# A hybrid attention and DeltaNet layer: the first attention unit's loads ahead of the last gates, bias rows in eight transfers, the output norm's power one part earlier, the gate rows' load pinned

## The chip, the cores and the metric

The kernel runs on one core of a Trainium2 chip. The metric is device time in microseconds (us), the median of three runs. An execution taken by the hardware profiler gives the trace from which all durations here are read. Engines: PE is TensorE (matmuls; PEld its weight loads), DVE is VectorE, ACT is ScalarE, POOL is GpSimd, and SP issues all the transfers.

## The reference

One layer over 2048 latent tokens and 256 context tokens, width 1024. One input projection feeds two branches that are merged at the end.

```
q, k, v, z  = NA projections ; o_na = softmax over (8 x 16 neighbourhood + 256 context keys), with a bias per head and offset
dq, dk, dv  = short conv, L2 norm, rotary ; o_dn, _ = gated delta rule, forward and backward, chunks of 64
u_na = (o_na * silu(z_na)) @ w_o_na
o_dn = rmsnorm(o_dn, dn_norm_w)
u_dn = (o_dn * silu(z_dn)) @ w_o_dn
y    = sigmoid(g_na) * u_na + sigmoid(g_dn) * u_dn
out  = x + gate * (y @ w_out)
```

## The kernel before

The work runs in stages. Projections, norms, the convolution and the triangular solves come first; their results go to DRAM tiles (names `d_...`). The last of the projections are the gates: `gate_units` multiplies a block of weights (`slots`) with all tokens (`hT`), squashes the sums on ACT (L207) and stores them to `d_g`. The last two gate blocks are done group by group of tokens in `gate_group(1)` to `gate_group(4)`. Between their matmuls run the first four steps of the DeltaNet scan (those of the context). When a group is done its part of `hT` is given back, and later pools lie in that memory.

After `gate_group(4)` a loop of 32 attention units begins, each for 128 queries of four heads. A unit computes scores by pairs of heads (`scores`, `scores_ctx`: L1051 adds the masks as a product with `mkr`, L1054 multiplies q with keys; L1068 on DVE adds the bias and takes the maximum; L1080 and L1083 on ACT exponentiate), turns the probabilities by PE (L1091, L1100) and multiplies with the values (L1111, L1115). The bias rows are in a DRAM tile `d_rp`, 16 shifted copies of the padded table, so that a plain two-dimensional read gives the right shift to each query; `load_bias` reads them for four heads with 32 transfers of 16 partitions.

One step of the scan is woven into each unit: `scan` is a generator, and `pump(chain, 1)` in the unit's code lets it run to its next `yield`, so five parts of it lie at fixed places in the unit. A step makes products with the state (L853), forms the new values (L857, L860, L871, copied to `cw` by L873), and updates the state (L867, L880, L883) and the output (L865, L882, L888). From the 17th latent step on both directions of a block of tokens are there: L865 adds the other direction's output, which lies in `os_`, and `dn_out` follows one step later. `dn_out` squares the block on ACT (L902), sums per head on DVE (L905, L906), raises to the power -1/2 on POOL (L908), multiplies by that on DVE (L909), transposes on PE (L913), multiplies by the gate rows `zd` on DVE (L914) and stores to `d_oz`. So `dn_out` lies in the last 15 units of the loop, and once after it.

The instructions of PE, and in the loop those of DVE, ACT and POOL, keep the order in which the code is written. SP's are placed by a scheduler, except where `keep_in_program_order` (`behind`) pins one against others pinned so. SP starts its transfers in that order, and each waits for the one eight before it, since eight semaphores go round. The order that matters most here, in `dn_out` and in the scan's step:

```
S.activation(ob, oa, AF.Square)
yield
V.reduce_sum(out=so, in_=ob, axis=AX.X)
V.tensor_scalar(out=so, in0=so, scalar1=4.0 / 64, scalar2=4.0 * EPS, op0=ALU.mult, op1=ALU.add)
G.tensor_tensor(out=ro, in0=so, in1=nh, op=ALU.pow)
V.tensor_tensor(out=oa, in0=oa, in1=ro.unsqueeze(2).to_broadcast([P, H, C]), op=ALU.mult)
yield
```

## Time and profile before

| what | value |
|---|---|
| median of 3 runs | 2374.77 us (2372.61 to 2375.72) |
| the profiled execution, its own time | 2373.14 us |
| its span, first to last instruction | 2371.4 us |
| PE busy in the span | 2162.9 us, 91% |
| mean granted TensorE clock, share of full speed | 0.959 |

The span is what the trace shows; 1.74 us of the execution's time lie outside it, and the median of the runs lies 1.63 us above that execution. Busy time is summed per engine; where PE is busy nearly all the time, its idle stretches and the stretches at the lower clock are what can be shortened. All times in the rows below are from the start of the span.

### The profile page before, as it was taken

To read this page: it belongs to the slowest core of one execution; us is meant where nothing else is said; L and a number is where in the kernel's file an instruction comes from. 1 tells how busy PE (TensorE), PEld (TensorE's weight loads), DVE (VectorE), ACT (ScalarE), POOL (GpSimd) and SP (SyncE) were. 2 spreads that over 40 slices of the span, in tenths; PEclk is the share of its full clock that TensorE was granted. 3 is DMA by queue.
4 is the path that set the end of the run, shared out by engine and by line. 5 is a ranking of instruction groups with operands and counts; after the bars stand their busy time and mean duration, and the time that the engine had idled before them with its cause. 6 is when DMAs were issued, how large, how long until landed. Compare 5 with 4: busy or idle time off the path is not lost.

```text
span 2371.4 us, 47485 instructions
## 1 busy us (share of the span) xinstructions
PE 2162.9 (91%) x18615; PEld 1814.3 (77%) x18615; DVE 1468.9 (62%) x2378; ACT 868.3 (37%) x2657; POOL 844.4 (36%) x712
## 2 busy tenths in 40 slices
PE   6999998998889999999999995899878876999999
PEld 2778777876667778999998874677766665889988
DVE  3736777559959969959679213666666774322222
ACT  4524343353433332344662113455444543211110
POOL 2514777644433112223432011211133334543442
PEclk8999999999999999999999997999888987999999
DMA  7323444665585252251443475777866664444342
GB/s 269 99 75 77 112 125 120 165 151 141 133 198 126 67 127 74 72 138 54 97 91 88 101 201 159 194 196 195 211 165 175 180 170 142 144 125 120 110 123 83
DMA packets 433480, 319.81 MB, mean 135 GB/s; under 512 B 200485, under 2 KB 361657, under 8 KB 432697
## 3 DMA queue, kind: packets, MB, share of 16 engines
q1 hardware_dynamic: 433256, 316.77, 50.3%
q8 instruction: 147, 2.41, 0.4%
q14 instruction: 77, 0.63, 0.1%
HBM read 206.24 MB, written 106.76 MB: 132 GB/s over the span
## 4 chain that ended last, share of the span: by engine, by line
PE 52%; DVE 18%; DMA 10%; POOL 8%; issue 7%; ACT 2%; SPq 2%; POOLq 0%; DVEq 0%; ACTq 0%
PE pd L181 19%; PE pf L1354 7%; PE pu L1343 7%; DVE Xs L584 6%; DVE tmp L582 6%; PE pd L731 5%; PE pw L1054 2%; PE pc L880 2%; PE pt L1091 1%; POOL rn L509 1%; PE pc L853 1%; POOL ro L908 1%; POOL xa L521 1%; PE po L1111 1%; PE pw L1051 1%
## 5 line engine op out<-in xcount | busy, mean ns | idle before, releaser
L181 PE MATMUL pd<-hT,slots 128*128 128x512 f32 (+1 forms) x3360 | 809.3, 395 | 1.9 <-ACT hT L321 1.6
L181 PEld LDWEIGHTS pd<-hT,slots 128*128 128x128 f32 x3360 | 617.0, 190 | 146.5 <-issue 3.8
L582 DVE TENSOR_TENSOR tmp<-Xs 128x236 f32<-128x236 f32 (+43 forms) x310 | 302.5, 976 | 36.8 <-DMA Xs<-d_X 28.1
L584 DVE TENSOR_TENSOR Xs<-Xs,tmp 128x236 f32<-128x236 f32 (+43 forms) x310 | 305.6, 986 | 8.4
L128 POOL TENSOR_TENSOR slots<-w_raw,slots 128x512 fp32r<-128x512 f32 (+1 forms) x76 | 114.1, 1501 | 379.8 <-ACT slots L127 379.7
L731 PE MATMUL pd<-slots,hT 128*128 128x256 f32 x1248 | 160.4, 288 | 0.0
L731 PE MATMUL pd<-wide,hT 128*128 128x256 f32 x1248 | 156.4, 287 | 2.4 <-ACT wide L127 1.4
L731 PEld LDWEIGHTS pd<-wide,hT 128*128 128x128 f32 x1248 | 153.6, 193 | 3.3 <-ACT wide L127 1.8
L731 PEld LDWEIGHTS pd<-slots,hT 128*128 128x128 f32 x1248 | 155.2, 191 | 0.0
L1344 DVE SCALAR_TENSOR_TENSOR gt<-gt,pu 128x256 f32<-128x256 f32 x120 | 46.5, 418 | 123.8 <-DMA gt<-d_g 65.3
L486 DVE SCALAR_TENSOR_TENSOR y<-raw,vT,y 128x512 f32<-128x512 f32 (+1 forms) x112 | 95.1, 860 | 25.5 <-ACT raw L474 21.4
L1068 DVE CUSTOM_DVE_ANT_1 pr<-pw,bias 128x288 f32<-128x288 f32 (+3 forms) x128 | 66.3, 553 | 69.5 <-PE pw L1054 69.5
L696 POOL TENSOR_TENSOR nrn<-nss,nhalf 128x8 f32<-128x8 f32 x34 | 71.5, 2102 | 104.8 <-DVE nss L695 104.8
L1080 ACT ACTIVATE pr<-pr,nm 128x288 f32<-128x288 f32 (+3 forms) x128 | 77.9, 609 | 81.3 <-DVE nm L1077 81.2
L207 ACT ACTIVATE zt<-pd 128x512 f32<-128x512 f32 x73 | 43.4, 594 | 150.7 <-PE pd L181 80.0
L1358 DVE SCALAR_TENSOR_TENSOR ckd<-pf,gate 128x512 f32<-128x512 f32 x32 | 22.0, 691 | 121.2 <-PE pf L1354 117.7
L1343 PE MATMUL pu<-ckq,OS 128*128 128x256 f32 x512 | 95.1, 284 | 0.9 <-DVE cv L1344 0.9
L1346 ACT CAST yh<-gt 128x256 fp32r<-128x256 f32 x60 | 24.3, 406 | 191.9 <-POOL gt L1345 191.9
L1345 POOL TENSOR_TENSOR gt<-gt 128x256 f32<-128x256 f32 x60 | 45.0, 750 | 126.3 <-DVE gt L1344 123.5
L1102 ACT COPY pTc<-pt 128x512 f32<-128x512 f32 x64 | 37.5, 586 | 137.9 <-PE pt L1100 137.9
L867 POOL TENSOR_TENSOR sd<-sd,gts 128x512 f32<-128x512 f32 x36 | 40.0, 1111 | 129.8 <-PE pc L853 121.9
L127 ACT CAST slots<-w_raw 128x512 fp32r<-128x512 f32 (+1 forms) x76 | 46.4, 611 | 106.6 <-DMA w_raw<-in_w_in_dram 85.1
(299 smaller groups left out, 4647.9 us busy)
## 6 DMA issues: line engine op xcount, KB each, us to landing
w_raw<-in_w_in_dram SPq DMA_DIRECT2D x92, 256.0 KB
ckq<-d_kq SPq DMA_DIRECT2D x64, 256.0 KB
gt<-d_g SPq DMA_DIRECT2D x60, 256.0 KB
d_g<-zt SPq DMA_DIRECT2D x41, 256.0 KB
d_X<-X SPq DMA_DIRECT2D x72, 128.0 KB
Xs<-d_X SPq DMA_DIRECT2D x18, 512.0 KB
cv<-d_v SPq DMA_DIRECT2D x72, 128.0 KB
cT<-d_T SPq DMA_DIRECT2D x72, 128.0 KB
```

The lines of the kernel that those rows point to most:

```text
L128: G.tensor_tensor(out=lo[:, j:j + 4, 0:n], in0=wr, in1=hi[:, j:j + 4, 0:n].bitcast(F32), op=ALU.subtract)
L181: PE.matmul(ps[0:n, 0:m], a[:, k, 0:n], h_part(g, z, k), start=k == 0 and i == 0, stop=k == KB - 1 and i == 2)
L486: V.scalar_tensor_tensor(out=y[:, 0:m], in0=raw[:, o + j - 1:o + j - 1 + m], scalar=tap(j), in1=y[:, 0:m], op0=ALU.mult, op1=ALU.add)
L582: V.tensor_tensor(out=tv, in0=X[r, piv, cols].unsqueeze(1).to_broadcast([8 * n, m, w]), in1=X[r, rows, piv].unsqueeze(2).to_broadcast([8 * ...
L584: V.tensor_tensor(out=X[r, rows, cols], in0=X[r, rows, cols], in1=tv, op=ALU.add)
L696: G.tensor_tensor(out=rn, in0=ss, in1=nhalf, op=ALU.pow)
L731: PE.matmul(ps[:, 256 * i:256 * i + 256], h[:, 256 * j + P * i:256 * j + P * i + P], w[:, :, part, k, :], start=k == 0 and n == 0, stop=k ...
L880: PE.matmul(p4[half[d], h, :], ld["ckd"][half[d], h, :], w[half[d], h, :], start=True, stop=True)
L1068: V.tensor_tensor_reduce(rc(self.e[u][:, 0:nk]), rc(pws[u][:, 0:nk]), biases[self.hg][:, 2 * pr + u, k0:k0 + self.nr, w0:w0 + w], 1.0, -3. ...
L1080: S.activation(e[:, 0:nk], e[:, 0:nk], AF.Exp, bias=nm[:, u:u + 1], accum_out=self.sums[:, hh, 0:1])
L1343: PE.matmul(ps, a, r[:, k, :], start=k == 0 and n == 0, stop=k == 3 and n == 2)
L1354: PE.matmul(ps, a[:, k, P * i:P * i + P], b[k, n], start=k == 0 and m == 0, stop=k == KB - 1 and m == 2)
```

## The change

Four edits.

1. The loads of the first attention unit (`load_q(0)`, the masks `k_mk`, `att_load(0)`, the context values `vc`) and the casts of q and masks are written ahead of `gate_group(4)`. q and masks use the staging tile `oa` (`raw0`) in place of `fwr`, which lies in memory that is given back only after the gates. The bias rows stay behind `gate_group(4)`.
2. `d_rp` gets longer rows, so that one transfer can take four heads: eight transfers of 16 x 4 x 752 elements in place of 32 of 16 x 752, for each half of the heads.
3. In `dn_out` the `yield` moves from ahead of the sum to behind the power: sum and power are done one part earlier, the multiplication stays. In the scan's step the addition L865 moves behind L867 (L868 and L866 in the changed kernel).
4. The load of `zd` is pinned in program order.

```diff
-    d_rp = dram.tile([16, RL + 47], F32, name="d_rp")
+    RW = RL + 8 * 47
+    d_rp = dram.tile([16, RW], F32, name="d_rp")
...
-                if i - CCH >= 16:
-                    G.tensor_tensor(out=tq.rearrange("p h e -> p (h e)"), in0=tq.rearrange("p h e -> p (h e)"), in1=os_[:, NCH - 1 - i], op=ALU.add)
                 yield
             G.tensor_tensor(out=sd, in0=sd, in1=gts[:, i].unsqueeze(2).to_broadcast([P, H, C]), op=ALU.mult)
+            if main and i - CCH >= 16:
+                G.tensor_tensor(out=tq.rearrange("p h e -> p (h e)"), in0=tq.rearrange("p h e -> p (h e)"), in1=os_[:, NCH - 1 - i], op=ALU.add)
...
-                    SP.dma_start(out=zd, in_=d_z[1, :, :, P * (i - CCH - 16):P * (i - CCH - 15)].rearrange("p q t -> q p t"))
+                    tc.keep_in_program_order(SP.dma_start(out=zd, in_=d_z[1, :, :, P * (i - CCH - 16):P * (i - CCH - 15)].rearrange("p q t -> q p t")))
...
             S.activation(ob, oa, AF.Square)
-            yield
             so = q2.tile([P, H], F32, name="so", bufs=2)
...
             G.tensor_tensor(out=ro, in0=so, in1=nh, op=ALU.pow)
+            yield
             V.tensor_tensor(out=oa, in0=oa, in1=ro.unsqueeze(2).to_broadcast([P, H, C]), op=ALU.mult)
...
-            for h in range(4):
-                for qr in range(8):
-                    if qr % 4 == 0:
-                        yield z
-                    o = ((4 * hg + h) * 23 + 7 - qr) * 47
-                    behind(SP.dma_start(out=z[16 * qr:16 * qr + 16, h].rearrange("q k w -> q (k w)"), in_=skew[:, o:o + 16 * 47]))
+            for qr in range(8):
+                yield z
+                o = (4 * hg * 23 + 7 - qr) * 47
+                rows = skew[:, o:o + 4 * 23 * 47].rearrange("q (h w) -> q h w", h=4)[:, :, 0:16 * 47]
+                behind(SP.dma_start(out=z[16 * qr:16 * qr + 16].rearrange("q h k w -> q h (k w)"), in_=rows))
...
+        q_split = load_q(0)
+        mkraw = ap_("fwr").rearrange("p b t -> p (b t)")[:, 0:432]
+        SP.dma_start(out=mkraw, in_=k_mk)
+        first = att_load(0)
+        SP.dma_start(out=vc, in_=d_nv[0:TC].rearrange("(b q) e -> q b e", q=P))
+        q_split()
+        mkr = aq.tile([P, 432], F32R, name="mkr")
+        S.copy(mkr, mkraw)
+        gate_group(4)
...
-        first = att_load(0)
-        SP.dma_start(out=vc, in_=d_nv[0:TC].rearrange("(b q) e -> q b e", q=P))
         bias_load = load_bias(0)
...
-        mkraw = ap_("fwr").rearrange("p a b -> p (a b)")[:, 0:432]
-        SP.dma_start(out=mkraw, in_=k_mk)
-        mkr = aq.tile([P, 432], F32R, name="mkr")
-        S.copy(mkr, mkraw)
-        load_q(0)()
```

What this does to the queues is seen at three places. The first is SP's queue at the end of the gates. Before, the masks and the first q stand behind all 32 bias transfers:

```order
L1019 DMA azt<-d_z 128x2x512
L213 DMA d_g<-co 128x512
L834 DMA cv<-d_v 64x512
L835 DMA cT<-d_T 64x512
L834 DMA cv<-d_v 64x512
L835 DMA cT<-d_T 64x512
L975 DMA bias<-d_rp 16x752 x2
L213 DMA d_g<-zd 128x512
L975 DMA bias<-d_rp 16x752 x30
L1221 DMA fwr<-in_k_mk_dram 128x432
L951 DMA fwr<-d_nq 128x2x256
L951 DMA fwr<-d_nk 128x2x256
```

In the changed kernel SP issues q and masks (L952, L1029, into `oa`) some twenty transfers earlier, ahead of the first unit's other loads:

```order
L836 DMA cT<-d_T 64x512
L952 DMA oa<-d_nq 128x2x256
L1029 DMA oa<-in_k_mk_dram 128x432
L214 DMA d_g<-ob 128x512
L1012 DMA azt<-d_z 128x2x512
L1017 DMA vt<-d_nv 96x1x256 x3
L1031 DMA vc<-d_nv 128x2x512
L837 DMA ckd<-d_kd 64x512 x2
```

And further on in the same queue, where the 32 transfers stood, it has eight, behind the first loads for later units:

```order
L1012 DMA azt<-d_z 128x2x512
L835 DMA cv<-d_v 64x512
L836 DMA cT<-d_T 64x512
L835 DMA cv<-d_v 64x512
L836 DMA cT<-d_T 64x512
L952 DMA fwr<-d_nk 128x2x256
L952 DMA fwr<-d_nq 128x2x256
L214 DMA d_g<-zd 128x512
L975 DMA bias<-d_rp 16x4x752 x8
L837 DMA ckd<-d_kd 64x512 x2
```

So the masks and q have moved ahead of the bias rows, and the bias rows stay last. The second place is DVE in a unit of the loop that has `dn_out` in it. Before, the sums L905 and L906 follow the maximum over the context keys (L1075, L1077):

```order
L857 TENSOR_TENSOR cr<-pc,egw 128x512
L1075 TENSOR_REDUCE mx<-pw 128x1 x2
L1077 TENSOR_REDUCE nm<-mx 128x2
L905 TENSOR_REDUCE so<-ob 128x8
L906 TENSOR_SCALAR so<-so 128x8
L909 TENSOR_TENSOR co<-co,ro 128x512
L914 SCALAR_TENSOR_TENSOR zd<-pc,vT,zd 128x512
```

In the changed kernel (line numbers 1 to 9 higher) they stand ahead of it:

```order
L858 TENSOR_TENSOR cr<-pc,egw 128x512
L905 TENSOR_REDUCE so<-ob 128x8
L906 TENSOR_SCALAR so<-so 128x8
L1084 TENSOR_REDUCE mx<-pw 128x1 x2
L1086 TENSOR_REDUCE nm<-mx 128x2
L910 TENSOR_TENSOR co<-co,ro 128x512
L915 SCALAR_TENSOR_TENSOR zd<-pc,vT,zd 128x512
```

Three small DVE instructions now come between the sums and the multiplication. The third place is POOL in the same unit. Before, the power L908 stands behind the scan's two operations:

```order
L1123 COPY rb<-ri 128x256
L865 TENSOR_TENSOR cr<-cr,OS 128x512
L867 TENSOR_TENSOR sd<-sd,gts 128x512
L908 TENSOR_TENSOR ro<-so,nh 128x8
L955 TENSOR_TENSOR ql<-fwr,qh 128x512
```

In the changed kernel it stands ahead of both, and these two have changed places:

```order
L1132 COPY rb<-ri 128x256
L908 TENSOR_TENSOR ro<-so,nh 128x8
L866 TENSOR_TENSOR sd<-sd,gts 128x512
L868 TENSOR_TENSOR cr<-cr,OS 128x512
L956 TENSOR_TENSOR ql<-fwr,qh 128x512
```

What followed the power directly, here a split of q (L955) or in other units nothing, has moved behind two operations more. PE's order is the same in both kernels up to the final projections. The load of `zd`, which before stood twice at the start of the loop and from then on was always two blocks ahead, now stands one block ahead, at the end of the step that makes the block.

## Rows read from the trace of the kernel before

**Rows 1.** The page, part 1: busy us (share of the span) and instructions

```profile
PE 2162.9 (91%) x18615; PEld 1814.3 (77%) x18615; DVE 1468.9 (62%) x2378; ACT 868.3 (37%) x2657; POOL 844.4 (36%) x712
```

**Rows 2.** Windows: stretch, length, busy us per engine, granted clock, DMA share, GB/s

```profile
1420.00:1447.00 27.00, 2.56 (x19) 1.52 (x13) 1.22 (x4) 1.17 (x2) 1.30 (x1) 0.58 0.55 152
1447.00:1705.00 258.00, 231.54 (x4247) 183.87 (x4249) 165.81 (x447) 124.49 (x365) 47.66 (x50) 0.91 0.73 192
1705.00:1980.00 275.00, 219.89 (x3939) 180.04 (x3934) 196.07 (x458) 128.77 (x361) 94.92 (x87) 0.90 0.66 172
```

**Rows 3.** Timeline of PE, end of gates: start, length, line, out<-in, [idle before <-releaser]

```profile
1418.98 1.15 PE L880 MATMUL pc<-cw,ckd 64*64 64x64 f32 x32
1443.70 0.85 PE L1051 MATMUL pw<-mkr 64*128 64x288 f32 x4 [23.57 <-ACT mkr L1223]
```

**Rows 4.** Timeline of SP's issues, same place

```profile
1414.17 0.59 SPq L1019 DMA_DIRECT2D azt<-d_z  x1
...
1425.68 0.34 SPq L213 DMA_DIRECT2D d_g<-zd  x1
1426.07 14.24 SPq L975 DMA_DIRECT2D bias<-d_rp  x30
```

**Rows 5.** Timelines of ACT and of DVE, same place

```profile
1443.10 0.55 ACT L1223 CAST mkr<-fwr 128x432 fp32r<-128x432 f32 x1 [23.41 <-DMA fwr<-in_k_mk_dram]
...
1446.47 0.46 DVE L1068 CUSTOM_DVE_ANT_1 pr<-pw,bias 128x288 f32<-128x288 f32 x1 [25.53 <-PE pw L1054]
```

**Rows 6.** Windows at the same place, for the last column, GB/s

```profile
1418.00:1422.00 4.00, 2.13 (x37) 1.53 (x35) 0.69 (x1) 0.60 (x1) 0.00 (x0) 1.00 0.87 247
...
1434.00:1438.00 4.00, 0.00 (x0) 0.00 (x0) 0.00 (x0) 0.00 (x0) 0.00 (x0) 0.50 0.39 108
```

**Rows 7.** Waits, 1705 to 1990 us: us in total, times, longest

```profile
PE pc L913 <- DVE co L909: 53.6, 15, 5.1
```

**Rows 8.** Timeline of PE in two units with `dn_out`

```profile
1829.30 0.61 PE L1115 MATMUL po<-pTc,vc 128*64 128x128 f32 x8
1833.97 1.12 PE L913 MATMUL pc<-ident,co 128*128 128x128 f32 x4 [4.06 <-DVE co L909]
...
1839.90 0.88 PE L1111 MATMUL po<-pT,vt 120*64 120x128 f32 x12
...
1886.78 0.66 PE L913 MATMUL pc<-ident,co 128*128 128x128 f32 x4 [2.95 <-DVE co L909]
...
1891.48 1.09 PE L1111 MATMUL po<-pT,vt 128*64 128x128 f32 x16
```

**Rows 9.** Timeline of DVE in the first of these units

```profile
1827.89 0.74 DVE L1075 TENSOR_REDUCE mx<-pw 128x1 f32<-128x256 f32 x2
...
1828.74 0.68 DVE L905 TENSOR_REDUCE so<-ob 128x8 f32<-128x512 f32 x1
1829.45 0.96 DVE L906 TENSOR_SCALAR so<-so 128x8 f32<-128x8 f32 x1
1832.17 1.74 DVE L909 TENSOR_TENSOR co<-co,ro 128x512 f32<-128x512 f32 x1 [1.76 <-POOL ro L908]
...
1836.45 0.17 DVE L1120 TENSOR_SCALAR ri<-ri 128x4 f32<-128x4 f32 x1
```

**Rows 10.** Timeline of POOL in that unit

```profile
1829.35 1.04 POOL L867 TENSOR_TENSOR sd<-sd,gts 128x512 f32<-128x512 f32 x1
1830.49 1.65 POOL L908 TENSOR_TENSOR ro<-so,nh 128x8 f32<-128x8 f32 x1
1832.11 1.26 POOL L955 TENSOR_TENSOR ql<-fwr,qh 128x512 fp32r<-128x512 f32 x1
```

**Rows 11.** Line L909: ns min/median/max over all 16, first and last start

```profile
L909 DVE TENSOR_TENSOR co<-co,ro x16: 691/692/1791, 1721.1 to 1993.0; 128x512 f32<-128x512 f32 x16
```

**Rows 12.** Timeline of POOL, an earlier power of the same shape, beside busy DVE

```profile
1102.87 2.51 POOL L696 TENSOR_TENSOR nrn<-nss,nhalf 128x8 f32<-128x8 f32 x1 [1.67 <-DVE nss L695]
```

**Rows 13.** SP's waits, 1705 to 1990 us: us in total, times, longest

```profile
SPq L894 <- DMA d_oz<-zd: 57.0, 14, 5.1
```

More of the change, by code (lines that the diff above doesn't have):

```diff
@@ L370, in body @@
         SP.dma_start(out=d_rp[0, 0:RL].rearrange("(h y x) -> y h x", h=8, x=47), in_=rz)
-        SP.dma_start(out=d_rp[0, RL:RL + 47], in_=rz[0:1, 0, :])
-        SP.dma_start(out=d_rp[1:16], in_=d_rp[0:1].to_broadcast([15, RL + 47]))
+        SP.dma_start(out=d_rp[0:1, RL:RW], in_=rz[0:1].rearrange("o h x -> o (h x)"))
+        SP.dma_start(out=d_rp[1:16], in_=d_rp[0:1].to_broadcast([15, RW]))
         hi, lo = take(O_BA, 32)
@@ L963, in load_rows @@
             return split_later(KH[:, :, c], KL[:, :, c], d_nk[2 * hg:2 * hg + 2, :, TC + 256 * g:TC + 256 * g + 256].rearrange("b q t -> q b t"))
-        skew = d_rp.rearrange("q l -> (q l)")[15:15 + 16 * (RL + 46)].rearrange("(q l) -> q l", l=RL + 46)
+        skew = d_rp.rearrange("q l -> (q l)")[15:15 + 16 * (RW - 1)].rearrange("(q l) -> q l", l=RW - 1)
         def load_bias(hg):
             z = ap.tile([P, 4, 16, 47], F32, name="bias", bufs=2)
-            for h in range(4):
-                for qr in range(8):
-                    if qr % 4 == 0:
-                        yield z
-                    o = ((4 * hg + h) * 23 + 7 - qr) * 47
-                    behind(SP.dma_start(out=z[16 * qr:16 * qr + 16, h].rearrange("q k w -> q (k w)"), in_=skew[:, o:o + 16 * 47]))
+            for qr in range(8):
[3 more added lines that the diff above has]
+                behind(SP.dma_start(out=z[16 * qr:16 * qr + 16].rearrange("q h k w -> q h (k w)"), in_=rows))
         order_pe = tc.manual_schedule(engines={mybir.EngineType.PE})
@@ L997, in body @@
         vc = aq.tile([P, 2, 512], F32, name="vc")
-        gate_group(4)
-        s1.close()
-        lp = pool("lp")
-        gate = lp.tile([P, D], F32, name="gate")
-        ap = pa_("ap")
-        ap_ = lambda name: ap.tile([P, 2, 256], F32, name=name, bufs=4)
-        pw = pa_("pw", 3, space=PSUM)
         rg_in, rg_z = {}, {}
@@ L1031, in load_q @@
             return split_later(*rg_in[n], d_nq[2 * hg:2 * hg + 2, :, 512 * rg + 128 * cg:512 * rg + 128 * cg + 256].rearrange("p q t -> q p t"))
+        q_split = load_q(0)
[7 more added lines that the diff above has]
+        gate_group(4)
+        s1.close()
+        lp = pool("lp")
+        gate = lp.tile([P, D], F32, name="gate")
+        ap = pa_("ap")
+        ap_ = lambda name: ap.tile([P, 2, 256], F32, name=name, bufs=4)
+        pw = pa_("pw", 3, space=PSUM)
         class Unit:
@@ L1291, in body @@
         pump(gprod, 1000)
-        s2k = lambda name, dt=F32: q2.tile([P, H, C], dt, name=name, bufs=1 if name in ("cr", "cw") else 2).rearrange("p h e -> p (h e)")
+        s2k = lambda name, dt=F32: q2.tile([P, H, C], dt, name=name, bufs={"cr": 1, "cw": 1}.get(name, 2)).rearrange("p h e -> p (h e)")
         oh, ol = {}, {}
```

## The prediction

> **What bounds the kernel now.** I read the page's busy shares first. PE is busy 91% of the span and DVE, the next, 62% [rows 1], so time is won where PE stands idle or runs at the lower clock. The windows by stage come next. Up to 1420 us the code is the same in both kernels. Then come three stretches that the change touches: 27 us in which PE works 2.6 us, 258 us of attention units without the output norm, in which PE is busy 231.5 us, and 275 us of units with it, in which PE is busy only 219.9 us [rows 2]. The reader should see that the third stretch has 55 us without PE work, about twice as many as the second, and that no other engine is near its limit there. I then asked who releases PE. In the 27 us it is one wait: the last work of the gates starts at 1418.98 and runs 1.15 us, and the masks' product starts at 1443.70, after 23.57 us of idleness that ends with the cast of the masks on ACT [rows 3]. In the third stretch nearly all of it is one line: the transposes L913 wait for the multiplication L909 on DVE, 15 times, 53.6 us in total, 3.57 us on the mean [rows 7].
>
> **First loads and bias rows (edits 1 and 2).** The masks' cast waits for the masks' transfer [rows 5], and that transfer stands in SP's queue behind the bias rows: 30 of the 32 issues take 14.24 us, 0.47 us each [rows 4]. While SP issues them the transfers move only 108 GB/s; four microseconds around the end of the gates show 247 GB/s [rows 6]. So the issuing sets the pace, not the moving. In the changed kernel q and masks are issued some twenty places earlier, their casts come ahead of the last gates' squashing on ACT, and PE can do the first scores at about 1420.2, directly behind L880. These four masks' products and six key products leave the path. What is late next is the bias: L1068 on DVE, which starts at 1446.47 now [rows 5], needs all eight new transfers, since each fills 16 partitions for all four heads. PE has the scores of the context keys behind it in the order, two of which need a buffer that L1068 frees, and then the scan's L853, so the start of L1068 is the measure of this part.
>
> When do the eight land? Now the store at 1425.68 is held until the second 512 KB `azt` load, issued at 1414.17, has landed [rows 4]: 11.5 us for one transfer in the crowd, the slowest I use. The q and mask loads put 256 + 216 = 472 KB more ahead of it, 2.0 us at 247 GB/s, so that point moves to 1427.6. Then there are 256 KB of keys, 256 KB of q, 256 KB of the last gate's store and 8 x 188 = 1504 KB of bias: 2272 KB, 9.4 us at 247 GB/s. L1068 would start at 1437.0, 9.4 us earlier. From both sides: if the bias itself moves at no more than 108 GB/s it takes 14.3 us behind 3.2 us for the rest, 1445.1, and the gain is 1.4 us. If neither the 472 KB nor the other loads are in its way it takes 6.2 us from 1425.7 on, and the gain is 14.5 us. I take 9, since the 108 is so plainly made by issues of 47 KB. The clock in this stretch falls to its lower level either way (0.58 on the mean [rows 2]) and comes back after work resumes, so I count nothing for it. The casts of q and masks stand ahead of a gate's squashing on ACT; they are covered as long as both loads land before that squashing is due, and if they are late the store of that gate is late by as much, while PE has other buffers to go on with. The bias for the other heads, three issues fewer in each of eight units, I cost at nothing, since SP is not what PE waits for there.
>
> **The power one part earlier (edit 3).** I follow one unit. PE ends L1115 at 1829.91 and starts L913 at 1833.97 [rows 8]. On DVE the sum L905 starts at 1828.74, behind the maximum L1075 that starts at 1827.89; L906, eight numbers per partition, takes 0.96 us although another operation of its kind and size takes 0.17 [rows 9]. It ends at 1830.41, when L867 on POOL ends (1829.35 + 1.04) [rows 10]. The power follows, 1.65 us from 1830.49, and L909 starts at 1832.17 and takes 1.74 us, beside a POOL operation of 1.26 us that starts at 1832.11 [rows 9, 10]. Over all units the median of L909 is 0.69 and the longest 1.79 [rows 11]: it is short where nothing runs beside it on POOL.
>
> After the change the sum starts where the maximum did, 1827.89. L906 starts 0.71 later, at 1828.60, and since L865 and L867 now stand behind the power, POOL is free and it takes 0.17: done 1828.77. The power starts 0.08 later, at 1828.85, and ends at 1830.50, 1.64 us earlier than now. L909 starts 0.03 later, at 1830.53, but now L867 starts beside it in every unit. With L955 beside it, L909 took 1.74 for 1.26, that is 0.48 more than its neighbour; with 1.04 beside it I get 1.52, end 1832.05, and L913 0.06 later at 1832.11. PE's gap is then 2.20 us. Fifteen such gaps are 33.0 us in place of 53.6: 20.6 us gained. From both sides: if L909 gets through first, at 0.69, the gap is 1.37 and the gain 33.0. If the power is stretched by DVE's work beside it, as an earlier one of the same shape was, 2.51 us [rows 12] in place of 1.65, the gap is 3.06 and the gain 7.7. I take the middle one: beside the power now run only two small reductions that read PSUM, and L867 starts before L909 in the pattern of the rows.
>
> [...]
>
> What is late next: the maximum's end moves back by the two sums, about 0.9 us, so ACT's exponentials end near 1831.8 and PE's L1091, which reads the first of them, comes behind L913, near 1832.7. That covers it. L865, and the splits behind it, end about 1.2 us later on POOL; their readers (L888, the next unit's scores) come late in the unit, behind PE's scores.
>
> **The clock after the gap.** With the gap of 4.06 us the stretch from L913 to the next L1111 takes 5.93 us; with the gap of 2.95 at 1886.78 it takes 4.70 [rows 8]. [...] So the clock costs 1.23 us in a unit where it falls, 18 us if it falls in all 15. A gap of 2.20 is shorter than both, and shorter than any of the 15. I take that the fall is spared in about six or seven units: 8 us, between 0 and 18.
>
> **The pinned load (edit 4).** SP waits 57.0 us in 14 pieces for the store of a block before it may load gate rows into the same buffer [rows 13]. One block ahead the load goes into the other buffer, so this wait goes. But PE waits for no transfer there, so I count nothing. It matters as cover: the third stretch moves 172 GB/s in 275 us [rows 2], 47.3 MB; 28.6 us shorter it needs 192 GB/s, just what the second stretch shows, and SP has the 57 us to give.
>
> **The sum.** 9 + 20.6 + 8 = 37.6 us off a span of 2371.4 gives 2333.8; with 1.74 us outside it 2335.5 for such an execution; the median of runs lies 1.63 higher: 2337 us. The bounds together would be 9 us (2366) and 65 us (2309).
>
> **Rivals.**
> First, POOL and DVE get in each other's way as at the lower bound: the power takes 2.5 us. For it speaks the 2.51 [rows 12]; against it, that there large DVE operations on SBUF ran beside. 9 + 7.7 + 2 for the clock gives 2356.
> Second, the larger bias transfers land no sooner. For it: they are behind the 472 KB, on the same crowded queue. Against it: 247 GB/s at the same place. 1.4 + 20.6 + 8 gives 2345.
> Third, hidden anyway: both of these at once, 9 to 11 us, 2364 to 2366.
> Fourth, slower than before: the gate rows, loaded one block ahead and no longer two, come late, and L914 waits in each of 15 units. Issued when one block's L914 is done, they have a unit's length to the next, (275 - 28.6) / 15, about 16 us. The longest landing in the rows is 11.5 us for twice the bytes [rows 4], so it should hold. Beyond 16 us each microsecond costs 15; from 18.5 us on it eats the whole gain, and at 20 us the time is 2374.8 - 37.6 + 60, about 2397.
>
> **How the numbers follow.** The sum as forecast, with L909, the clock and the bias each somewhere between its bounds: 0.68, and 2320 to 2350 for it. First rival 0.13, second 0.12, third 0.04, late gate rows 0.03. The range 2320 to 2354 leaves out most of the first rival, the third, the fourth and the case where the clock never falls and L909 goes first, about 2 in 10. About 0.2%, 4.7 us, is what a measurement of this kernel can tell from no change. All cases but the fourth are faster by more; for a transfer or a wait that I have not seen and that eats the smaller gains I leave 0.03 to no change. Faster 0.94, same 0.03, slower 0.03.
>
> **What would show it.** L1051 should start near 1420 and L1068 near 1437. In units with the norm L906 should take about 0.17 us, the power start near 1.6 us earlier against L857, L909 take 1.5 us beside L867, and PE wait near 2.2 us ahead of L913, 33 us in all. The granted clock of those units should rise above 0.90, and SP's wait of 57 us should be gone. The prediction is wrong if a new wait stands ahead of L913 or L914, if the power grows, or if L1068 waits for its bias beyond 1443.

## The result

The changed kernel takes 2349.15 us, median of 4 runs (2345.65 to 2356.83), beside 2375.19 us for the kernel before (2372.61 to 2375.72). The ratio is 0.9897, with an interval of [0.9871, 0.9922]: about 26 us faster. The prediction was 2337 us with a range of 2320 to 2354. The time lies in the range, 12 us above the number, and not all of the reasons held.

The page of the changed kernel, first part (columns as in [rows 1]), and its second half of units. By this I mean, here and below, the time from the 16th to the 32nd start of the copy `rb` on POOL (L1123 before, L1132 after), 16 units with the same 4164 matmuls in every kernel. The windows show that stretch after the change:

```profile
PE 2153.9 (92%) x18615; PEld 1805.2 (77%) x18615; DVE 1472.6 (63%) x2378; ACT 868.0 (37%) x2657; POOL 847.3 (36%) x712
1689.21:1957.26 268.05, 228.53 (x4164) 185.05 (x4164) 205.96 (x486) 133.37 (x374) 98.92 (x90) 0.92 0.74 188
```

The same stretch in the kernel before:

```profile
1693.32:1981.62 288.30, 232.33 (x4164) 189.98 (x4164) 206.09 (x486) 133.22 (x374) 95.31 (x89) 0.89 0.66 172
```

In these two profiles the second half is 20.25 us shorter. PE's idle time fell from 55.97 to 39.52 us, and its busy time by 3.8 us, at a mean granted clock of 0.92 in place of 0.89. The waits of PE in the changed stretch, three rows that answer to [rows 7], and below them two of SP's queue, where the 57.0 us for the store [rows 13] are gone and waits for `vt` are left:

```profile
PE pc L914 <- DVE co L910: 29.1, 15, 2.2
PE po L1120 <- DMA vt<-d_nv: 2.8, 2, 1.4
PE pc L883 <- DVE zd L915: 2.1, 1, 2.1
```

```profile
SPq L916 <- DMA vt<-d_nv: 8.5, 6, 2.4
SPq L895 <- DMA vt<-d_nv: 7.9, 6, 2.4
```

One unit of it on PE, on DVE and on POOL, as in [rows 8 to 10]:

```profile
1820.61 0.66 PE L914 MATMUL pc<-ident,co 128*128 128x128 f32 x4 [2.21 <-DVE co L910]
```

```profile
1816.39 0.68 DVE L905 TENSOR_REDUCE so<-ob 128x8 f32<-128x512 f32 x1
1817.10 0.17 DVE L906 TENSOR_SCALAR so<-so 128x8 f32<-128x8 f32 x1
...
1819.03 1.52 DVE L910 TENSOR_TENSOR co<-co,ro 128x512 f32<-128x512 f32 x1 [0.91 <-POOL ro L908]
```

```profile
1817.35 1.65 POOL L908 TENSOR_TENSOR ro<-so,nh 128x8 f32<-128x8 f32 x1 [8.95 <-DMA ckd<-d_kd]
1818.96 1.04 POOL L866 TENSOR_TENSOR sd<-sd,gts 128x512 f32<-128x512 f32 x1
1819.96 1.73 POOL L868 TENSOR_TENSOR cr<-cr,OS 128x512 f32<-128x512 f32 x1
```

The reader is to see the forecast of edit 3 here nearly to the hundredth: L906 takes 0.17, L910 takes 1.52 beside L866, and PE's gap is 2.21. The unit is typical: over all 15, L906 takes 0.17, the power 1.65 and L910 1.52 to 1.53.

At the boundary the picture is another. PE after the change, then SP and DVE, as in [rows 3 to 5]:

```profile
1416.40 1.15 PE L881 MATMUL pc<-cw,ckd 64*64 64x64 f32 x32
1417.48 0.52 PE L1060 MATMUL pw<-mkr 64*128 64x288 f32 x4
...
1442.00 0.58 PE L1063 MATMUL pw<-KHc,qh 64*128 64x256 f32 x1 [23.48 <-DVE mx L1077]
```

```profile
1425.02 6.20 SPq L975 DMA_DIRECT2D bias<-d_rp  x8
```

```profile
1441.45 0.46 DVE L1077 CUSTOM_DVE_ANT_1 pr<-pw,bias 128x288 f32<-128x288 f32 x1 [23.10 <-DMA ckd<-d_kd]
```

The scores come early, as forecast, and then PE waits 23.48 us for the bias. The eight transfers are issued by 1431.22, and the first addition starts at 1441.45. (The row names a load of `ckd` as the releaser; L1077 does not read it, what it needs are the bias rows.) Windows over that wait, whose last three columns are clock, share of the DMA engines and GB/s, as in [rows 6]:

```profile
1426.00:1430.00 4.00, 0.00 (x0) 0.00 (x0) 0.00 (x0) 0.00 (x0) 0.00 (x0) 0.50 1.02 154
1430.00:1434.00 4.00, 0.00 (x0) 0.00 (x0) 0.00 (x0) 0.00 (x0) 0.00 (x0) 0.50 1.08 134
1434.00:1438.00 4.00, 0.00 (x0) 0.00 (x0) 0.00 (x0) 0.00 (x0) 0.00 (x0) 0.50 1.05 132
```

The DMA engines count as busy the whole time (1.02 to 1.08) and move 132 to 154 GB/s, all transfers together. Before, they were busy for 0.39 of the time and moved 108 [rows 6].

### The profile page after: what moved, and what is told of

The parts are those of the page before. It is cut to its first block, busy times and chain, and to the rows that moved or that the text cites. A ratio compares the mean times of both kernels' runs of the same rounds, so it can differ in the third digit from the quotient of the medians.

```text
span 2345.3 us, 47416 instructions
## 1 busy us (share of the span) xinstructions
PE 2153.9 (92%) x18615; PEld 1805.2 (77%) x18615; DVE 1472.6 (63%) x2378; ACT 868.0 (37%) x2657; POOL 847.3 (36%) x712
## 4 chain that ended last, share of the span: by engine, by line
PE 48%; DVE 18%; DMA 12%; issue 9%; POOL 7%; ACT 3%; SPq 2%; DVEq 0%; POOLq 0%; ACTq 0%
PE pd L182 19%; PE pf L1356 7%; PE pu L1345 7%; DVE Xs L585 6%; DVE tmp L583 5%; PE pd L732 5%; DMA vt<-d_nv 2%; POOL rn L510 1%; PE pw L1063 1%; PE pc L881 1%; POOL xa L522 1%; POOL ro L908 1%; POOL nrn L697 1%; POOL kd L530 1%; DMA d_v<-xT 1%
## 5 line engine op out<-in xcount | busy, mean ns | idle before, releaser
L487 DVE SCALAR_TENSOR_TENSOR y<-raw,vT,y 128x512 f32<-128x512 f32 (+1 forms) x112 | 95.4, 863 | 24.5 <-ACT raw L475 20.9
L1077 DVE CUSTOM_DVE_ANT_1 pr<-pw,bias 128x288 f32<-128x288 f32 (+3 forms) x128 | 66.1, 553 | 59.7 <-PE pw L1063 36.3
L866 POOL TENSOR_TENSOR sd<-sd,gts 128x512 f32<-128x512 f32 x36 | 40.2, 1117 | 150.8 <-PE pc L854 121.7
```

What stands on the lines that cost most here:

```text
L487: V.scalar_tensor_tensor(out=y[:, 0:m], in0=raw[:, o + j - 1:o + j - 1 + m], scalar=tap(j), in1=y[:, 0:m], op0=ALU.mult, op1=ALU.add)
L1077: V.tensor_tensor_reduce(rc(self.e[u][:, 0:nk]), rc(pws[u][:, 0:nk]), biases[self.hg][:, 2 * pr + u, k0:k0 + self.nr, w0:w0 + w], 1.0, -3. ...
```

## The experiments

For each kernel the profile gives four lengths: from the start of the gates' last matmuls (L880 or L881) to the first addition of the bias (a) and to the first `rb` (b), from the first to the 16th `rb` (c), and the second half (d). The last column is the ratio of the times to the kernel before on the same chip, 4 to 12 runs of each kernel; not all rows come from one chip, so rows are compared by this ratio. The start of the gates' last matmuls itself lies between 1416.4 and 1422.1 us in these profiles. The program up to there is the same but for the copies of the bias table, so one profile is good to some 3 us, and small things are read from lengths and not from the span.

| kernel | a | b | c | d | ratio, interval |
|---|---|---|---|---|---|
| before | 27.49 | 38.41 | 235.93 | 288.30 | 1 |
| the change | 25.05 | 35.91 | 236.90 | 268.05 | 0.9897 [0.9871, 0.9922] |
| the change again | 24.80 | 36.60 | 240.77 | 265.44 | 0.9886 [0.9869, 0.9903] |
| edit 3 alone | 27.35 | 38.91 | 237.86 | 280.54 | 0.9943 [0.9927, 0.9958] |
| edit 1 alone | 14.66 | 31.63 | 236.06 | 290.26 | 0.9957 [0.9941, 0.9972] |
| edit 2 alone | 26.04 | 36.91 | 239.74 | 292.45 | 1.0001 [0.9990, 1.0011] |
| edit 4 alone | 26.72 | 37.88 | 233.51 | 292.06 | 0.9999 [0.9988, 1.0010] |
| edits 3, 4 | 27.05 | 37.87 | 236.04 | 267.98 | 0.9879 [0.9855, 0.9903] |
| edits 1, 2, 3 | 25.87 | 37.62 | 238.45 | 282.25 | 0.9958 [0.9945, 0.9972] |
| edits 1, 3, 4 (32 transfers) | 14.46 | 31.41 | 235.59 | 265.70 | 0.9856 [0.9840, 0.9873] |
| 16 transfers | 18.38 | 30.07 | 234.09 | 262.62 | 0.9859 [0.9840, 0.9879] |
| 4 transfers | 14.60 | 28.56 | 238.64 | 269.33 | 0.9861 [0.9842, 0.9881] |
| POOL moved | 24.59 | 35.45 | 240.10 | 260.36 | 0.9883 [0.9866, 0.9901] |
| POOL moved, 16 transfers | 20.25 | 31.65 | 238.06 | 261.28 | 0.9818 [0.9798, 0.9837] |

**Edit 3 alone.** The kernel before with this:

```diff
-                if i - CCH >= 16:
-                    G.tensor_tensor(out=tq..., in1=os_[:, NCH - 1 - i], op=ALU.add)
                 yield
             G.tensor_tensor(out=sd, in0=sd, in1=gts...)
+            if main and i - CCH >= 16:
+                G.tensor_tensor(out=tq..., in1=os_[:, NCH - 1 - i], op=ALU.add)
...
             S.activation(ob, oa, AF.Square)
-            yield
...
             G.tensor_tensor(out=ro, in0=so, in1=nh, op=ALU.pow)
+            yield
```

> The kernel before with edit 3 alone (the power one part earlier, the addition L865 behind L867). Theory: the power carries nearly the whole result. The wait of L913 falls from 53.6 us to about 29, as in the changed kernel, and the time is 2349 to 2352. Rival: the power only works together with the pinned gate rows, because SP's 57 us wait for the stores holds back the transfers that a shorter unit needs; then vt, azt or gate rows come late, about half of the gain goes into new transfer waits, and the time is about 2362.

Measured: 2363.83 us beside 2378.04, ratio 0.9943. The rival was right. PE's two largest waits and SP's largest in its second half:

```profile
PE po L1111 <- DMA vt<-d_nv: 25.9, 15, 4.0
PE pc L913 <- DVE co L909: 16.9, 11, 2.2
```

```profile
SPq L894 <- DMA d_oz<-zd: 56.7, 14, 5.5
```

The wait for the multiplication falls to 16.9 us, lower than in the changed kernel, but PE now stands 25.9 us before the values matmuls, for `vt`, for which it never waits in the second half of the kernel before. Edit 3 alone gives about half.

**Edits 1, 2 and 3, without the pin.**

```diff
-                    tc.keep_in_program_order(SP.dma_start(out=zd, in_=d_z[1, ...]))
+                    SP.dma_start(out=zd, in_=d_z[1, ...])
```

> The changed kernel without edit 4: the gate rows' load goes back to the place that the scheduler gives it, two blocks ahead, where it waits on SP for a block's store. Theory: PE waits for no transfer that the pin helps, so the pin is worth nothing or costs a little: the new waits of PE for vt at 1631 to 1671 us and the one wait for the gate rows at 1731 us (about 5 us) go away, and the time is 2344 to 2350. Rival: the pin is what makes the shorter units possible; without it SP's wait of some 57 us comes back, later loads stand behind it, and the time is 2354 or more.

Measured: 2367.95 beside 2378.04, ratio 0.9958. The theory fell, the rival held. The same waits in its second half:

```profile
PE po L1120 <- DMA vt<-d_nv: 21.4, 14, 2.6
PE pc L914 <- DVE co L910: 18.3, 10, 2.2
```

```profile
SPq L895 <- DMA d_oz<-zd: 55.9, 14, 5.7
```

And one place on SP: the load of gate rows is held until the store of the block before last has landed, and the three loads of `vt` stand five issues behind it in the same queue.

```profile
1827.07 0.54 SPq L916 DMA_DIRECT2D d_oz<-zd  x1
1831.73 0.37 SPq L895 DMA_DIRECT2D zd<-d_z  x1
...
1833.98 0.59 SPq L839 DMA_DIRECT2D cA<-d_A  x1
1834.67 2.27 SPq L1017 DMA_DIRECT2D vt<-d_nv  x3
```

In the same unit of the changed kernel these issues stand in the same order, but the load of gate rows follows the issue of the store by 1.42 us in place of 4.12. Over all the units it is 0.04 to 2.5 us there and 3.6 to 6.5 here. So it is the hold, and not another order, that delays `vt`:

```profile
1809.88 0.38 SPq L916 DMA_DIRECT2D d_oz<-zd  x1
1811.68 0.37 SPq L895 DMA_DIRECT2D zd<-d_z  x1
```

**Edit 4 alone.** The kernel before with the pin.

> The kernel before with edit 4 alone (gate rows' load pinned where the program has it). Theory: before the change PE's long wait ahead of L913 hides what the pin helps: without the power edit vt is not late (no wait of PE for it in the second half of the units), so the pin alone is worth nothing, and the time is within 4 us of before; the second half of the units (from the 16th to the 32nd copy rb) stays near 288 us. Rival: the pin gives its 14 us (282 against 268 us with the other edits) in any surroundings; the second half takes about 275 us, and the time is 2361 to 2365.

Measured: 2376.12 beside 2377.11, ratio 0.9999, second half 292.06: the theory held. PE's wait ahead of L913 is 51.4 us, and there is one wait for `vt` in all units, of 2.0 us. So the pin's gain needs the shorter gap: as long as PE stands 3.57 us on the mean ahead of L913, `vt` is there in time with the hold and without it.

**Edits 3 and 4.** The kernel before with the two diffs above.

> The kernel before with edits 3 and 4 alone (power one part earlier, gate rows' load pinned). Theory: the pin is worth nothing alone and takes away the power's transfer waits when both are there, so the two together give nearly the whole result: PE's waits for vt in the second half are 5 us or less in place of the 25.9 of the power alone, the second half of the units takes 265 to 270 us, and the ratio to before is 0.989 to 0.992. Rival: the pin only helps with the loads issued earlier at the boundary (edit 1), and the second half stays near 280 us, ratio 0.994.

Measured: 2347.32 beside 2376.49, ratio 0.9879, second half 267.98: the theory held. PE's first two waits there:

```profile
PE pc L913 <- DVE co L909: 28.0, 13, 2.2
PE po L1111 <- DMA vt<-d_nv: 3.6, 2, 1.8
```

So edit 3 alone is worth 14 us, edit 4 alone nothing, both 29. This is already all that the full change gives: edits 1 and 2 together add nothing that these runs can tell.

**Edit 1 alone.** The early block of loads, with the bias rows in 32 transfers and nothing else:

```diff
+        q_split = load_q(0)
...
+        SP.dma_start(out=mkraw, in_=k_mk)
+        first = att_load(0)
...
         gate_group(4)
...
-        first = att_load(0)
...
-        load_q(0)()
```

> The kernel before with edit 1 alone (q, masks, keys and the first unit's other loads issued ahead of the last gates; the bias rows still in 32 transfers). Theory: what ends the wait at the boundary is the moving of the bias rows, and the number of their issues does not matter; then edit 1 alone gives what the changed kernel shows there: L1077 (the line that is L1068 before) starts 2 to 4 us earlier behind the gates' last L880, 24 to 25.5 us behind it, and the time is 2370 to 2373. Rival: the issues do matter (32 x 0.47 us = 15 us), L1077 starts 27 us or more behind L880 as before, and the time is 2374 to 2377.

Measured: 2367.04 beside 2378.04, ratio 0.9957. Neither theory foresaw it: L1077 starts 14.66 us behind L880, 10.4 us earlier than in the changed kernel. DVE's additions of the bias in the first unit show why:

```profile
1433.93 0.46 DVE L1077 CUSTOM_DVE_ANT_1 pr<-pw,bias 128x288 f32<-128x288 f32 x1 [12.71 <-DMA bias<-d_rp]
...
1438.08 0.46 DVE L1077 CUSTOM_DVE_ANT_1 pr<-pw,bias 128x288 f32<-128x288 f32 x1 [1.98 <-DMA bias<-d_rp]
...
1442.51 0.46 DVE L1077 CUSTOM_DVE_ANT_1 pr<-pw,bias 128x288 f32<-128x288 f32 x1 [1.60 <-DMA bias<-d_rp]
...
1446.22 0.46 DVE L1077 CUSTOM_DVE_ANT_1 pr<-pw,bias 128x288 f32<-128x288 f32 x1 [3.24 <-DMA bias<-d_rp]
```

The four heads come one by one, some 4.1 us apart: eight transfers of 47 KB in 4.1 us. The last head comes 26.95 us behind L880, later than all of them in the changed kernel (25.05), but the first comes 10.4 us earlier, and work on it fills a part of the waits for the others. This led to a third theory: the rate of moving is much the same in 8 and in 32 transfers, and what edit 2 loses is the order by heads. The issues of this run, on SP:

```profile
1427.51 16.91 SPq L975 DMA_DIRECT2D bias<-d_rp  x32
```

None of the 32 waits for a bias transfer, and each head's first addition starts 1.8 to 1.9 us behind the end of its eighth issue. No transfers pile up behind the issues here, so in 32 transfers the pace is still that of the issuing, some 4 us for the eight issues of a head.

**Edit 2 alone.** The kernel before with `load_bias` and `d_rp` of the change.

> The kernel before with edit 2 alone (the bias rows in 8 transfers of 188 KB in place of 32 of 47 KB), masks and q behind them in the queue as before. Theory: the moving is the limit, so the last bias row lands as late as before, but SP is free to issue masks and q 10 us earlier; these two share the engines with the bias rows. L1068 starts 25 to 28 us behind the gates' last L880, and the time is within 3 us of before, 2372 to 2376. Rival: the issues are the limit; L1068 starts 18 to 20 us behind L880, and the time is 2366 or less.

Measured: 2377.93 beside 2378.04, ratio 1.0001; L1068 starts 26.04 us behind L880, and the theory held. SP has issued the eight by 1431.21, nine microseconds sooner than the 32 [rows 4], and nothing comes of it.

**Edits 1, 3 and 4, the bias rows in 32 transfers.**

```diff
-            for qr in range(8):
...
-                behind(SP.dma_start(out=z[16 * qr:16 * qr + 16]..., in_=rows))
+            for h in range(4):
+                for qr in range(8):
...
+                    behind(SP.dma_start(out=z[16 * qr:16 * qr + 16, h]..., in_=skew[:, o:o + 16 * 47]))
```

> The changed kernel with edit 2 undone (edits 1, 3 and 4 stay; the bias rows go in 32 transfers, head by head, as before). Theory: the first addition of the bias, L1077, needs only the rows of its own head; in 8 transfers that each hold a part of all four heads it must wait for the last byte, in 32 it waits for the first eight. As in the run with edit 1 alone, L1077 starts about 15 us behind the gates' last L881 in place of 25, and the first unit's L1132 (the copy rb) stands 4 to 5 us earlier against L881 (31.6 in place of 35.9). The time is 4 to 5 us under the changed kernel's, ratio to before 0.987 to 0.989. Rival: it is lost again in the units that follow, which are paced by transfers; the time equals the changed kernel's.

Measured: 2343.50 beside 2377.11, ratio 0.9856; L1077 starts 14.46 us behind L880, and b is 31.41. The theory held: without edit 2 the change is faster, by 0.3 to 0.4% (0.9856 against 0.9886 and 0.9897; the intervals overlap by a little).

**Sixteen transfers, two heads at a time.**

```diff
+            for h in (0, 2):
+                for qr in range(8):
...
+                    behind(SP.dma_start(out=z[16 * qr:16 * qr + 16, h:h + 2]..., in_=rows))
```

> The changed kernel with its bias rows in 16 transfers of 94 KB, the first two heads ahead of the other two. Theory: what matters is which head's rows land first, and the moving keeps its some 92 GB/s (1504 KB in 16.4 us in the changed kernel). Heads 0 and 1 are then complete 8 to 9 us behind the first issue, L1077 starts 17 to 18 us behind the gates' last L881, and the first unit's L1132 stands some 31 to 33 us behind it: the time is within 2 us of that with 32 transfers. Rival: fewer issues make the moving faster (16 x 0.5 = 8 us for all of it); then L1132 stands 28 us or less behind L881, and the time is 4 us or more under that with 32.

Measured: 2341.82 beside 2377.11, ratio 0.9859. The first addition starts 18.38 us behind L881, 10.2 us behind the first issue, a little later than the theory had it, and b is 30.07, a little better. The time is that of 32 transfers, as the theory said; half the issues did not make the moving faster. The eighth issue ends at 1435.91 and the first addition starts 3.8 us later, so in this form the moving lags behind the issuing.

**Four transfers, one head to all 128 partitions.**

```diff
-    d_rp = dram.tile([16, RW], F32, name="d_rp")
+    d_rp = dram.tile([23, RL + 47], F32, name="d_rp")
...
+            for h in range(4):
...
+                rows = bass.AP(at.tensor, at.offset, [[RL, 8], [RL + 46, 16], [1, 16 * 47]])
+                behind(SP.dma_start(out=z[:, h].rearrange("q k w -> q (k w)"), in_=rows))
```

> The changed kernel with its bias rows in 4 transfers, one for each head, each of 376 KB to all 128 partitions (the DRAM copy has 23 rows in place of 16, so that one address pattern reaches all partitions; what is computed is the same). Theory A: what slows the eight transfers is that each writes only 16 partitions; to all 128 the rows move at the 247 GB/s of the rows of before, head by head: L1077 starts 11 to 13 us behind the gates' last L881, the fourth head lands 7 to 8 us behind the first issue, L1132 stands 26 to 28 us behind L881, and the time is 8 to 10 us under the changed kernel's, ratio 0.985 to 0.987. Theory B: it is the reading of these rows in DRAM that is slow: the four take 16 us as now, 4 us each, L1077 starts about 15 us behind L881, and the time is that of 32 transfers.

Measured: 2342.40 beside 2377.11, ratio 0.9861, and b 28.56, the shortest. The first two heads on DVE, and the windows:

```profile
1436.08 0.46 DVE L1076 CUSTOM_DVE_ANT_1 pr<-pw,bias 128x288 f32<-128x288 f32 x1 [12.64 <-DMA bias<-d_rp]
...
1438.69 0.46 DVE L1076 CUSTOM_DVE_ANT_1 pr<-pw,bias 128x288 f32<-128x288 f32 x1 [2.15 <-DMA bias<-d_rp]
```

```profile
1434.00:1438.00 4.00, 1.40 (x21) 1.18 (x25) 0.47 (x2) 0.00 (x0) 0.00 (x0) 0.50 0.62 181
1438.00:1442.00 4.00, 2.71 (x66) 2.34 (x58) 2.93 (x8) 1.86 (x8) 1.04 (x1) 0.50 0.61 225
```

The same rows, read in the same runs of 3008 bytes, now move with the engines busy for 0.61 of the time while all transfers together move 181 to 225 GB/s; eight transfers to 16 partitions each kept them busy all the time (1.02 to 1.08) at 132 to 154. The first two heads land 2.6 us apart, 376 KB each, 148 GB/s; the other two are there before PE has their scores. So the runs fit theory A in kind: four transfers to all 128 partitions each moved these rows faster than eight to 16 each. (The four transfers also have another source pattern and are fewer; these runs do not separate that from the partitions.) In size it holds by half, since 247 GB/s is not reached and the time does not tell the four from the 32 or the 16. Theory B, that the reading is slow, falls.

**The change again, and POOL's work moved from beside L910.** In the units with the norm, L866 goes ahead of the power's inputs and L868 behind `rb`:

```diff
             V.tensor_tensor(out=r, in0=r, in1=grown(0, egs[:, i]), op=ALU.subtract)
+            late = main and i - CCH >= 16
+            if late:
+                G.tensor_tensor(out=sd, in0=sd, in1=gts...)
             yield
...
             S.copy(w, p2)
             yield
+            if late:
+                G.tensor_tensor(out=tq..., in1=os_[:, NCH - 1 - i], op=ALU.add)
```

> The changed kernel once more, so that the next two and it stand beside each other on one chip: ratio to before 0.988 to 0.992. The second half of its units (from the 16th to the 32nd copy rb) takes about 268 us, with 15 gaps of 2.0 to 2.2 us ahead of the transposes L914.

> The changed kernel with the two additions and products on POOL that stand behind the power (L866, L868) taken away from beside L910 in the units with the norm: L866 goes one part up, ahead of the power's inputs, L868 behind the copy rb; what is computed is the same. Theory: L910's 1.52 us is 0.69 of its own plus the time for which POOL's L866 and L868 hold it up; alone it takes 0.69, PE's gap ahead of L914 falls from 2.20 to 1.37 us, the sum of 15 from 33 to 21, and the time is 8 to 14 us under the changed kernel's (more where the shorter gap also spares the clock its fall). Rival 1: the addition L868, now behind rb, comes late for L889, and the wait goes to the end of the unit: same time as the changed kernel. Rival 2: the splits L956 step into the place beside L910 in every second unit, and the gain is half, 4 to 6 us.

Measured: the change again 2350.58 beside 2378.67, ratio 0.9886; POOL moved 2348.68, ratio 0.9883. A unit of the second, DVE and PE, and its second half:

```profile
1825.72 0.69 DVE L914 TENSOR_TENSOR co<-co,ro 128x512 f32<-128x512 f32 x1 [0.91 <-POOL ro L912]
...
1828.29 1.07 DVE L1132 TENSOR_TENSOR ri<-sums 128x4 f32<-128x4 f32 x1
```

```profile
1826.46 0.66 PE L918 MATMUL pc<-ident,co 128*128 128x128 f32 x4 [1.36 <-DVE co L914]
...
1829.40 0.43 PE L1067 MATMUL pw<-KH,ql 64*128 64x360 f32 x2 [0.75 <-POOL ql L960]
```

```profile
1697.65:1958.01 260.36, 221.05 (x4164) 176.06 (x4164) 196.51 (x486) 132.18 (x374) 92.47 (x89) 0.98 0.76 192
```

The multiplication (L914 here) takes 0.69 in 14 of the 15 units, and the gap is 1.36, as the lower bound of the prediction had it. PE's wait there falls from 32.1 us in 15 pieces (the change again) to 19.3 in 13, the clock rises from 0.93 to 0.98, and the second half is 5.1 us shorter. Nearly all of the 5.1 is PE's busy time, 4.4 us less at the higher clock; PE's idle time is 39.3 us and was 40.0. What the gaps gave is taken back elsewhere: PE now waits 5.7 us, 7 times, for the splits of q on POOL, 4.2 us, twice, for L919 on DVE, which in three units waits for gate rows (9.8 us), and 3.2 us for `vt`. The small sum L1132 takes 1.07, beside POOL's split of 1.27, where elsewhere it takes 0.15. The time does not show the 5 us: the two ratios are the same within their intervals. Neither the theory's 8 to 14 us nor half of it came in the time. Rival 1's wait is there but small, 3.9 us on DVE for the addition behind `rb`; the splits of rival 2 come late for PE and do not stand beside the multiplication.

**POOL moved, and 16 transfers.** Both edits above.

> The changed kernel with the bias rows in 16 transfers by pairs of heads and with L866 and L868 taken from beside L910. Theory: the two gains are at different places and add: 7 to 9 us from the bias and 8 to 14 us from L910, ratio to before 0.980 to 0.983. Rival: the transfers of the second half (already 190 GB/s) hold the units back, and it is no faster than with the 16 transfers alone, ratio 0.986.

Measured: 2336.57 beside 2378.67, ratio 0.9818, the fastest of all these kernels and faster than the change by more than the intervals. It lies 0.4% under the 16 transfers alone, so here moving POOL's work does pay, though the second halves (261.28 and 262.62) hardly differ. The profile of this kernel is of its slowest execution, 2341.17 us, so its lengths do not show the gain of the median. The 16 transfers alone ran on another chip. Why it pays here in the time and not with the eight transfers stays open.

## Why the prediction was right, and where it was not

**First loads and bias rows: 9 us forecast, 2.4 measured** (a: 27.49 to 25.05). The scores came ahead as said (L1060 at 1417.48, 1.08 us behind the start of L881), and L1077 at 1441.45 was still inside the bound of 1443, but near its bad end. The step that failed is the 247 GB/s for the bias, which I drew from "So the issuing sets the pace, not the moving". For the 32 transfers that reading stands: none of their issues waits for a bias transfer (edit 1 alone), and eight of 47 KB in 4.1 us are 94 GB/s. But it does not follow that fewer issues move faster. In 8 transfers the moving sets the pace, at the same rate: all are issued by 1431.22, the first addition starts 10.2 us later, and 1504 KB from the first issue at 1425.02 to 1441.45 are 94 GB/s again. The second limit lay just behind the first, and nothing in [rows 6] shows it. So the second rival's 1.4 us describes this part better than my 9. The four transfers to 128 partitions show how far this goes: 148 GB/s between their first two heads, with the engines busy for 0.61 and 0.62 of the time, where the eight to 16 partitions each moved 94 with the engines busy for 1.02 to 1.08.

What I had in hand and did not weigh is the sentence that L1068 "needs all eight new transfers, since each fills 16 partitions for all four heads". With masks and q early, the first head's rows are what the first unit waits for, and in 32 transfers they land 10 us sooner. I costed the merging only by its issues. Alone, edit 2 is worth nothing; behind edit 1 it takes back what edit 1 gives: with edits 1, 3 and 4, the three kernels in which the first heads land first lie at 0.9856 to 0.9861, the change with its eight transfers at 0.9886 and 0.9897.

**The power one part earlier: 20.6 us forecast, 24.5 measured on the wait itself** (53.6 to 29.1). Two of the 15 gaps, 0.58 and 0.61 us, are short because PE had just waited for `vt`; without these two the saving is about 21, the forecast. L906, the power and L910 took what the sum said. The whole idle time of PE fell only by 16.45 us, since 6 us came as new waits, for `vt`, once behind `zd`, and small ones, and 2 us in pieces too short for the rows. So this term is right by its steps and about 4 us too large in what is left of it.

**The clock: 8 us forecast, 3.8 measured in these two profiles, 8.6 between all** (PE busy 232.33 to 228.53). One profile of each is too few: over the same 4164 matmuls the four kernels that keep the long gap show 232.2 to 235.9 us (mean 234.1), the six with gaps of about 2.1 and the pin 222.4 to 228.5 (mean 225.5; 225.48 in the change again). It is spared in part, as said. The price of 1.23 us in a unit fits the granted clock of its two stretches in the kernel before: 0.74 on the mean over the 5.93 us, 1.00 over the 4.70. At the gap of 1.36 us the mean clock is 0.98 and PE's busy time 221.05: some of this term was still to be had.

**The pinned load: "so I count nothing".** This was the wrong step that mattered most. I read from the kernel before that PE waits for no transfer there, which is true, and took it over to units that are shorter. The pin is worth nothing before, and some 15 us after edit 3 (29 against 14 us; 0.9958 against 0.9886 in the full change). The reasoning one line further on, that the shorter stretch needs 192 GB/s and that SP has the 57 us to give, held the answer: the 57 us had to be given, or `vt` would come late. That the number came out well is because the kernel had the pin.

**The other terms.** The 9 + 20.6 + 8 became 2.5 at the boundary (b) and 20.25 in the second half, minus 1.0 in the first half (c), 21.8 in all; the remaining 4.3 of the 26.1 us by which the span is shorter lie ahead of the gates' end (2.6 us, in code that is the same there) and behind the last unit (1.7). This remainder looks like scatter of single profiles: between the means of the four kernels with the long gap (288.3 to 292.5) and of the six with the short one and the pin (262.6 to 269.3) the second half is 24.3 us shorter, and with the 2.5 at the boundary that is 26.8, the whole. So of the 11.6 us that the forecast has too much, some 6.5 are the bias and 4 the waits that came new in the second half. The fourth rival, late gate rows, happened in part: DVE waited for them once, 5.2 us, and in the change again three times, 5.2 us together, of which PE lost 2.1 us in the first and nothing that the rows show in the second. The power was not stretched (1.65), against the first rival.

## What to carry to other kernels

Before an edit that shortens a loop is costed, look for the waits of the issuing queue that the long loop hides: here the load that waits for a store (55.9 us in 14 pieces without the pin) holds back the loads behind it, and PE waits 21.4 us for `vt` when the gap over it has become shorter. When transfers are merged, ask first which bytes the next instruction needs: the eight that each hold a part of all four heads let the first addition start 25.05 us behind the start of the gates' last matmuls, the 32 by heads 14.46. Ask also how many partitions each merged transfer writes: the rows moved at 94 GB/s in eight transfers to 16 each, and at 148 in four to 128. A pair of edits of which one is worth nothing alone is tested with both, since here neither edit 3 nor edit 4 shows alone what the two are worth.

## What the runs showed of the hardware

Eight transfers in flight that together fill all 128 partitions, 16 each, moved no faster than 32 small ones issued one by one: 94 GB/s from first issue to first use, with the DMA engines counted as busy all the time (1.02 to 1.08, and 0.42 to 0.43 in the 32 of edit 1 alone).

In four pairs of operations DVE and POOL held each other up. L910 takes 0.69 alone (POOL moved) and 1.52 beside L866 and L868; L868 takes 1.73 beside it and 1.28 alone (POOL moved); and there the sum of 4 numbers per partition, L1132, which starts at 1828.29 and takes 1.07 us, ends together with the split on POOL:

```profile
1828.08 1.27 POOL L960 TENSOR_TENSOR ql<-fwr,qh 128x512 fp32r<-128x512 f32 x1 [2.39 <-ACT qh L959]
```

In these pairs whichever came second ended when the first had ended and its own length had passed, but for about 0.14 us. L910 ends 0.55 us behind L866 in all 15 units (0.69 alone), L868 1.13 to 1.14 behind L910 (1.27 to 1.28 alone), L906 0.03 behind L867 in the kernel before (0.17 alone), and the small sum 0.02 behind the split (0.15 alone). That is why the prediction's 1.52, worked out from such a pair (1.74 beside 1.26), came out.

PE's mean granted clock in the second half is 0.87 to 0.89 in the kernels with gaps of mostly 2.9 to 5.1 us ahead of the transposes, 0.92 to 0.94 with gaps of about 2.1 (0.90 and 0.92 where PE also waits for `vt` in most units), and 0.97 and 0.98 with 1.3 to 1.4 (a few gaps apart). Windows inside one level show 0.50 (1426 to 1438 us after the change) or 1.00. The gap does not set the clock alone. The same unit, behind the same gap of 2.13 us, ran from L914 to the values matmuls at a mean clock of 0.74 in the change and at 1.00 in the change again, first row and second:

```profile
1855.00:1861.61 6.61, 6.61 (x96) 5.09 (x97) 5.42 (x12) 2.98 (x6) 4.90 (x6) 0.74 0.91 210
1857.59:1862.91 5.32, 5.32 (x96) 4.20 (x96) 3.87 (x11) 3.07 (x6) 4.91 (x6) 1.00 0.49 135
```

The 1.29 us between them is the price of a fall, near the 1.23 of the prediction.
